# Two decoder layers on one core: output weights split ahead of the last gate and into dead tiles of the heads, the last gate by halves of its contraction, the early pool kept open

## The chip, the cores and the metric

The kernel runs on one core of a Trainium2 chip. The metric is the time of one execution in microseconds (us) on the device; the lower the better.

## What is computed

A trunk of two layers over 1024 tokens of width 1024, in float32. Each layer is `h = h + rmsnorm(mixer(rmsnorm(h)))`, and each mixer ends in a gate and an output projection:

```python
# layer 0: 16 heads of 64 in each of three dilated window groups
y = o.reshape(B, S, DIL_WIDTH).astype(h.dtype) * jax.nn.silu(gate)
return y @ w_out
# layer 1: 8 differential heads, v of width 128
y = o.reshape(B, S, DIFF_WIDTH) * jax.nn.silu(gate)
return y @ w_out
```

The part of interest is the turn at each layer's end: the last gate projection, the last heads, `y @ w_out`, and the norm behind it.

## The kernel before

**Numbers.** A float32 product is made of three matmuls: each operand is split into a high part (a ScalarE cast, `split`, L184) and a low part (a subtraction on VectorE or GpSimd in turn, `low`, L122). XH and XL, 128 x 8 x 1024, hold the transposed activations' high and low parts; slice kt is the kt-th 128 rows of the contraction (eight slices).

**Filler.** The heads run step by step, and between their steps `fill.at` lets a generator issue projection work: the projections of later heads (qk), then the late gates (`late_gates`, psum banks tagged "pj"), then `out_early`. TensorE's order is thus written out in the program; on the other engines, SyncE's list of transfers among them, a scheduler sets it by its own times. SyncE ("SP") issues every transfer, in one queue, in order.

**out_early.** Once the last gate has read XH and XL, finished branch outputs y are loaded over them (`load_y`, from the DRAM tensor y_d). With kt 0 to 3 (EARLY = 4) there, the first half of the output projection runs for eight token blocks n in two halves c, 12 matmuls each, in psum tiles `pe`. Each `pe` is copied by ScalarE into the tile `part`, which is stored over the slices of XH and XL that it has used up. The last two blocks (n = 6 and 7; HELD = 2) come after the last head. Then `po` takes kt 4 to 6 for block 0, for blocks 1 and 2, and at last kt 7 and the norm block by block (`out_rest`). Weights of kt are loaded into `raw` (two buffers), then split: kt 0 to 2 and 4 to 6 into the three buffers of `w_tiles` (tags "wh", "wl"; tiles print as wh and wl), kt 3 into "rh" of the early pool, kt 7 into a pool of its own (both print as owh and owl).

**What a turn waits for.** kt 0 to 2 share their three buffers with the weights of the last gates, and kt 4 to 6 share them with kt 0 to 2, so they can be split only when the last `pe` has been issued. In layer 0 the last y (`combine`) comes out of the softmax denominators by a chain: st_d, js, wt_d, twelve loads `wb`, the products on VectorE, the casts to XH and XL.

Of the kernel before, what the change touches and what calls it, by code (L numbers as in the profile page):

```python
# [10 lines left out]
F32 = mybir.dt.float32  # L11
# [81 lines left out]
def trunk(ctx: ExitStack, tc: tile.TileContext, a: dict, out: bass.AP):  # L93
# [177 lines left out]
    def project(o, wh, wl, tok):  # L271
        k = 0
        for kt in range(KT):
            for l, r_ in ((wh, XH), (wh, XL), (wl, XH)):
                nc.tensor.matmul(o, lhsT=l[:, kt, :], rhs=r_[:, kt, tok], start=k == 0, stop=k == 3 * KT - 1)  # L275
                k += 1
                yield 512

    def gate_units(pool, layer, w, fs, eng=None):
# [21 lines left out]
    def late_gates(pool, layer, w, fs):  # L301

        s = pool.tile([P, len(fs), T], F32, tag="r", name="sil", bufs=3 - layer)
        for v in gate_units(pool, layer, w, fs):
# [51 lines left out]

    stored = set()
# [28 lines left out]
    def out_weights(w, kt, tiles):  # L386
        raw = raw_tile([P, D])
        nc.sync.dma_start(raw, w[ts(kt), :])
        split(*tiles, raw)
        return tiles  # L390

# [11 lines left out]
    def out_early(pool, layer, w, held):  # L403

        ws = []
        for kt in range(EARLY):
            while (layer, kt) not in stored:
                yield None
            load_y(layer, kt)
            tiles = w_tiles([P, D]) if kt < 3 else [  # L410
                pool.tile([P, D], F32R, tag="rh", name=t) for t in ("owh", "owl")]
            ws.append(out_weights(w, kt, tiles))
        for n in range(NB):
            t = pool.tile([P, D], F32, tag="r", name="part", bufs=3 - layer)
            for c in range(2):
# [8 lines left out]
                nc.scalar.copy(t[:, ts(c, 512)], bank)  # L424
            for c, o in enumerate(partial(n)):
                nc.sync.dma_start(o, quarters(t[:, ts(c, 512)]))
        for kt in range(EARLY, KT - 1):
            held[kt] = out_weights(w, kt, w_tiles([P, D]))
        banks = held["banks"] = out_banks(0)
        for kt in range(EARLY, KT - 1):  # L430
# [3 lines left out]
            yield from out_block(0, banks, kt, *held[kt], kt == EARLY, False)  # L434

    def out_rest(pool, w, held, finish, early=None):

        held[KT - 1] = out_weights(
            w, KT - 1, [pool.tile([P, D], F32R, tag=t, name=t) for t in ("owh", "owl")])
# [88 lines left out]
    early0 = tc.tile_pool(name="early0", bufs=2, side="right")  # L528
    with tc.tile_pool(name="l0", bufs=2) as lp, early0 as ep:
# [196 lines left out]
        def filler0():  # L726
            for i, (pr, g) in enumerate(units):
                yield from qk_unit(ep, i, a["dil_qk"][i], SUB[g])
            if LATE0:
                yield from late_gates(ep, 0, a["dil_g"], range(8 - LATE0, 8))  # L730
# [12 lines left out]
        for i in range(nst + LAG_P):  # L743
            if i < nst:
# [10 lines left out]
                hd.scores(c)  # L755
                fill.at((3 * i + 1) / 24)
# [18 lines left out]
    with tc.tile_pool(name="ow0", bufs=1, side="right", reuse_waits="tile") as owp, \  # L775
            tc.tile_pool(name="o0", bufs=2, reuse_waits="tile") as op:
# [10 lines left out]
        def values1(pool, v2, weights=(wp, ("wh", "wl")), **kw):  # L787

            for parts in v_weights(*weights, a["diff_v"][v2], 256, 4, nc.vector):
# [20 lines left out]
        with tc.tile_pool(name="v1", bufs=3) as vp:  # L810
            ones = keep.tile([P, 1], F32, name="ones")
            nc.vector.memset(ones, 1.0)
            subln = keep.tile([P, 1], F32, name="subln")
            nc.sync.dma_start(subln, a["diff_subln"][0].rearrange("(d o) -> d o", o=1))
            nc.vector.tensor_scalar_mul(subln, subln, (1.0 - LAMBDA_INIT) * SQ_SHIFT)

            lqk = []
            for nm_ in ("q1", "k1", "q2", "k2"):
                t = vp.tile([P, HD], F32, tag="l" + nm_, name="l" + nm_, bufs=1)
                nc.sync.dma_start(t, a["diff_lambda_" + nm_][0].partition_broadcast(P))  # L820
                lqk.append(t)
            lsum = vp.tile([P, 2], F32, tag="lsum", name="lsum", bufs=1)
            for i in range(2):
                nc.vector.tensor_tensor_reduce(
                    lqk[2 * i], lqk[2 * i], lqk[2 * i + 1], 1.0, 0.0, ALU.mult, ALU.add, lsum[:, i : i + 1])
            nc.scalar.activation(lsum, lsum, AF.Exp)
            neg_lam = keep.tile([P, 1], F32, name="neg_lam")
            nc.vector.tensor_sub(neg_lam, lsum[:, 0:1], lsum[:, 1:2])
            nc.vector.tensor_scalar(neg_lam, neg_lam, LAMBDA_INIT, -1.0, ALU.add, ALU.mult)


            v = values1(vp, 0, (vp, ("vwh", "vwl")), tag="v")

            def first_weights():
                next(v)
                next(v)

            last = out_rest(owp, a["dil_w_out"][0], held, finish0, first_weights)
# [232 lines left out]
```

## Time and profile before

| | |
|---|---|
| median of three runs | 2046.3 us (2044.1 to 2049.32) |
| profiled execution, its own time | 2049.16 us |
| its span, first to last instruction | 2047.3 us |
| TensorE busy | 1911.4 us, 93% of the span |
| VectorE, ScalarE, GpSimd busy | 56%, 43%, 30% |
| mean granted TensorE clock | 0.975 of 2.4 GHz |

The difference of 1.9 us between the execution's time and its span lies outside the instructions. Where TensorE is busy nearly all the time, the stretches in which it isn't are those to read: slice 24 of 40 (1177 to 1228 us) shows 6 tenths, and the last ones 8.

### The profile page before, as it was taken

Reading aid. Unit: us, or ns where it says so; the run is one execution under the profiler, and the core shown is the slowest. Engines: PE = TensorE matmul, PEld = TensorE weight load, DVE = VectorE, ACT = ScalarE, POOL = GpSimd, SP = SyncE. Lnnn points to the kernel's source line nnn. Section 1 sums busy time; section 2 is a strip of 40 time slices with the busy share of each in tenths; the row PEclk is TensorE's granted clock in tenths of the full one; section 3 lists DMA queues with packets and bytes.
Section 4 is the critical chain, followed back from the end, with each engine's and each line's share of the span. In section 5 each row is a group of like instructions: output and inputs, shape, how many; then the busy total and the mean of one; then the engine's idle time right before and its main releaser. Section 6 shows DMA issues by size and latency. Waiting matters only on the chain.

```text
span 2047.3 us, 28864 instructions
## 1 busy us (share of the span) xinstructions
PE 1911.4 (93%) x10008; PEld 1598.6 (78%) x10008; DVE 1145.4 (56%) x2771; ACT 886.6 (43%) x2055; POOL 617.5 (30%) x386
## 2 busy tenths in 40 slices
PE   6999999999999999999999969899999899999888
PEld 4788888888787787788787848688879788887776
DVE  3311122146776767676767655570066877777626
ACT  3312122135555555555555555341245455546522
POOL 2000000143443434353535330230561534433121
PEclk8999999999999999999999979899999999999999
DMA  5424244277696969696969697542446565555643
GB/s 207 145 93 138 99 146 161 102 222 231 198 298 192 296 190 304 182 301 191 299 197 297 195 328 227 183 172 97 142 154 190 165 196 162 195 183 177 239 155 124
DMA packets 218018, 397.90 MB, mean 194 GB/s; under 512 B 40976, under 2 KB 123408, under 8 KB 217872
## 3 DMA queue, kind: packets, MB, share of 16 engines
q1 hardware_dynamic: 217872, 396.04, 60.7%
q8 instruction: 80, 1.31, 0.3%
q14 instruction: 66, 0.54, 0.1%
HBM read 254.87 MB, written 132.71 MB: 189 GB/s over the span
## 4 chain that ended last, share of the span: by engine, by line
PE 67%; DVE 11%; DMA 10%; ACT 4%; POOL 3%; issue 3%; SPq 1%; POOLq 0%; DVEq 0%; ACTq 0%
PE pqk L275 25%; PE pv L213 16%; PE pg L275 7%; PE po L377 3%; PE sc L576 3%; DMA wb<-wt_d 2%; PE sc L894 2%; PE up L626 2%; PE pe L420 2%; PE tp L599 2%; PE ob L945 2%; DVE u L649 1%; DMA st_d<-st 1%; POOL r L252 1%; DVE pm L897 1%
## 5 line engine op out<-in xcount | busy, mean ns | idle before, releaser
L275 PE MATMUL pqk<-XL,wh 128*128 128x512 f32 x1024 | 423.1, 413 | 0.0
L275 PE MATMUL pqk<-XH,wl 128*128 128x512 f32 x1024 | 411.8, 402 | 0.0
L275 PE MATMUL pqk<-XH,wh 128*128 128x512 f32 x1024 | 410.7, 401 | 0.9 <-DVE t L251 0.9
L122 POOL TENSOR_TENSOR wl<-raw,wh 128x1024 fp32r<-128x1024 f32 x41 | 98.5, 2402 | 612.1 <-ACT wh L184 612.1
L586 ACT ACTIVATE pm<-pm,st 128x128 f32<-128x128 f32 (+1 forms) x384 | 170.2, 444 | 155.9 <-DVE st L583 154.0
L275 PEld LDWEIGHTS pqk<-XH,wh 128*128 128x128 f32 x1024 | 194.9, 190 | 30.4 <-DVE t L251 1.9
L275 PEld LDWEIGHTS pqk<-XL,wh 128*128 128x128 f32 x1024 | 195.3, 191 | 27.6
L275 PEld LDWEIGHTS pqk<-XH,wl 128*128 128x128 f32 x1024 | 195.6, 191 | 27.2
L213 PE MATMUL pv<-vwh,XH 128*128 128x512 f32 (+1 forms) x448 | 173.8, 388 | 8.3 <-ACT XH L158 4.6
L250 POOL TENSOR_TENSOR r<-t 128x512 f32<-128x512 f32 x64 | 98.1, 1533 | 270.2 <-DVE t L249 269.2
L213 PE MATMUL pv<-vwl,XH 128*128 128x512 f32 (+1 forms) x448 | 172.4, 385 | 2.8 <-POOL vwl L122 2.8
L213 PE MATMUL pv<-vwh,XL 128*128 128x512 f32 (+1 forms) x448 | 172.6, 385 | 1.4 <-DVE XL L122 0.8
L184 ACT CAST wh<-raw 128x1024 fp32r<-128x1024 f32 x98 | 102.5, 1047 | 151.6 <-PE pqk L275 73.3
L122 DVE TENSOR_TENSOR wl<-raw,wh 128x1024 fp32r<-128x1024 f32 x57 | 76.0, 1333 | 147.6 <-ACT wh L184 147.3
L122 DVE TENSOR_TENSOR vs<-pv,vs 128x512 fp32r<-128x512 f32 x64 | 44.1, 689 | 200.5 <-ACT vs L495 187.9
L904 ACT ACTIVATE pm<-pm,mx 128x256 f32<-128x256 f32 (+7 forms) x128 | 99.4, 777 | 123.2 <-DVE mx L903 64.8
L122 DVE TENSOR_TENSOR pp<-tp,pp 128x512 fp32r<-128x512 f32 (+2 forms) x192 | 104.0, 541 | 80.8 <-ACT pp L603 79.2
L599 PE MATMUL tp<-ident,pm 128*128 128x128 f32 x560 | 96.3, 281 | 39.8 <-DVE pp L122 39.5
L599 PEld LDWEIGHTS tp<-ident,pm 128*128 128x128 f32 x560 | 73.1, 144 | 73.1 <-issue 36.5
L583 DVE CUSTOM_DVE_ANT_0 pm<-sc,masks 128x128 f32<-128x128 f32 (+1 forms) x384 | 118.7, 343 | 17.1 <-PE sc L576 15.7
L897 DVE CUSTOM_DVE_ANT_0 pm<-sc,md 128x512 f32<-128x512 f32 (+3 forms) x192 | 102.7, 551 | 31.1 <-PE sc L894 28.6
L495 ACT CAST vs<-pv 128x512 fp32r<-128x512 f32 x48 | 28.1, 586 | 187.2 <-PE pv L213 187.2
(516 smaller groups left out, 4441.0 us busy)
## 6 DMA issues: line engine op xcount, KB each, us to landing
qk_d<-rh SPq DMA_DIRECT2D x64, 512.0 KB
qk_d<-r SPq DMA_DIRECT2D x64, 512.0 KB
qh<-qk_d SPq DMA_DIRECT2D x128, 256.0 KB
ql<-qk_d SPq DMA_DIRECT2D x128, 256.0 KB
ka<-qk_d SPq DMA_DIRECT2D x64, 512.0 KB
v_d<-vs SPq DMA_DIRECT2D x48, 512.0 KB
raw<-in_dil_qk_dram SPq DMA_DIRECT2D x48, 512.0 KB
vt<-v_d SPq DMA_DIRECT2D x48, 512.0 KB
```

Source lines behind the costliest of these rows:

```text
L122: eng.tensor_tensor(o, full, hi.bitcast(F32), ALU.subtract)
L184: nc.scalar.copy(wh, raw)
L213: nc.tensor.matmul(o, lhsT=l, rhs=r_, start=first and k == 0, stop=last and k == 3 * KT - 1, skip_group_check=True)
L250: nc.gpsimd.tensor_sub(put(r[0]), nat(t1), nat(t2))
L275: nc.tensor.matmul(o, lhsT=l[:, kt, :], rhs=r_[:, kt, tok], start=k == 0, stop=k == 3 * KT - 1)
L377: nc.tensor.matmul(banks[c], lhsT=l[:, kt, ts(n)], rhs=r_[:, ts(c, 512)], start=first and k == 0, stop=last and k == 2,)
L576: nc.tensor.matmul(sc[:, cols], lhsT=q[:, ts(b)], rhs=kv, start=k == 0, stop=k == 1)
L583: nc.vector.tensor_tensor_reduce(pm[:, cols], sc[:, cols], m[:, m.shape[1] - w_ :], 1.0, 3.0e38, ALU.add, ALU.min, st[:, 0, j : j + 1])
L586: nc.scalar.activation(pm[:, cols], pm[:, cols], AF.Exp, bias=st[:, 0, j : j + 1], scale=-1.0, accum_out=st[:, 1, j : j + 1])
L599: nc.tensor.transpose(out=tp[:, ts(n)], in_=self.pb.pop((b, kb)), identity=ident)
L897: nc.vector.tensor_tensor_reduce(pm[:, k0:k1], sc[:, :w_], m_, 1.0, 3.0e38, ALU.add, ALU.min, mx[:, j : j + 1])
L904: nc.scalar.activation(pm[:, :wq], pm[:, :wq], AF.Exp, bias=mx[:, 0:1], scale=-1.0, accum_out=den)
```

## The change

1. `gate_units` opens both psum banks for the last gate f = 7 and projects kt 0 to 3 into both, then kt 4 to 7 into both (before: bank c = 0 over all kt, then c = 1). The number of matmuls is the same.
2. `prepare` issues loads and splits of the output weights kt 0 to 2 right behind the last gate's own split; kt 3 follows behind the gate.
3. `out_weights` picks tiles by kt: kt 0, 1, 3, 7 from `w_tiles`; kt 2 in the two "rh", kt 4 in "qh" and "ql", kt 5 in two "r", kt 6 in the two "ka" of the early pool, where the heads kept their operands. kt 4 to 6 are traced in front of block n = 6, once the last head's scores are issued; kt 7 behind the `pe` loop.
4. `part` is a tile of half the size, 128 x 512, with tag "t" (three buffers in layer 0, two in layer 1), in place of 128 x 1024 of tag "r".
5. The pools of kt 7 are gone; the early pool of layer 0 stays open till the first block of layer 1's values (`values1(0)`) is done, which takes its tiles from "pq" and `w_tiles`. The lambda of layer 1 is set up behind that, in the gates' stage.

```diff
+    def project(o, wh, wl, tok, kts=range(KT)):
...
+    def gate_units(pool, layer, w, fs, eng=None, prepare=None):
...
+            if prepare and f == fs[-1]:
+                prepare()
+                banks = [ps.tile([P, 512], F32, tag="pj", name="pg") for _ in range(2)]
+                for k0 in (0, EARLY):
+                    for c in range(2):
+                        yield from project(banks[c], wh, wl, ts(c, 512), range(k0, k0 + EARLY))
+                for c in range(2):
+                    yield f, c, banks[c]
+                return
...
+    def out_weights(pool, w, kt):
+
+        tags = {2: ("rh", "rh"), 4: ("qh", "ql"), 5: ("r", "r"), 6: ("ka", "ka")}
+        if kt in tags:
+            tiles = [pool.tile([P, D], F32 if t == "r" else F32R, tag=t, name="ow", bufs=2 if t != "r" else r_bufs[pool])
+                     for t in tags[kt]]
+            tiles = [t.bitcast(F32R) for t in tiles] if kt == 5 else tiles
+        else:
+            tiles = w_tiles([P, D])
         raw = raw_tile([P, D])
         nc.sync.dma_start(raw, w[ts(kt), :])
         split(*tiles, raw)
         return tiles
...
+    def out_early(pool, layer, w, ws):
+
+        ws[EARLY - 1] = out_weights(pool, w, EARLY - 1)
         for kt in range(EARLY):
             while (layer, kt) not in stored:
                 yield None
             load_y(layer, kt)
-            tiles = w_tiles([P, D]) if kt < 3 else [
-                pool.tile([P, D], F32R, tag="rh", name=t) for t in ("owh", "owl")]
-            ws.append(out_weights(w, kt, tiles))
         for n in range(NB):
-            t = pool.tile([P, D], F32, tag="r", name="part", bufs=3 - layer)
+            if n == NB - HELD:
+                while ("heads", layer) not in written:
+                    yield None
+                for kt in range(EARLY, KT - 1):
+                    ws[kt] = out_weights(pool, w, kt)
+            parts = []
...
-                nc.scalar.copy(t[:, ts(c, 512)], bank)
-            for c, o in enumerate(partial(n)):
-                nc.sync.dma_start(o, quarters(t[:, ts(c, 512)]))
-        for kt in range(EARLY, KT - 1):
-            held[kt] = out_weights(w, kt, w_tiles([P, D]))
-        banks = held["banks"] = out_banks(0)
+                t = pool.tile([P, 512], F32, tag="t", name="part", bufs=3 - layer)
+                nc.scalar.copy(t, bank)
+                parts.append(t)
+            for o, t in zip(partial(n), parts):
+                nc.sync.dma_start(o, quarters(t))
+        ws[KT - 1] = out_weights(pool, w, KT - 1)
+        banks = ws["banks"] = out_banks(0)
```

Three places show how the instructions move. In each row stand the line, the operation and out<-in with the buffer's number; "waits" lists the engines and transfer slots (DMAHW) whose work it waits for.

**Layer 0, SyncE, the y loads of kt 0 to 3.** Before, the first load (XH, kt 0) stands three rows ahead of this piece, and the weights of kt 2 (raw_11122) stand among the loads:

```order
L549 DMA vt_10878<-v0_d_59 128x4x128 [waits DMAHW3_49]
L394 DMA XL_79<-y_d0_63 128x1024 [waits DMAHW4_49]
L717 DMA sil_in_10861<-sil_d0_65 128x512 [waits DMAHW5_49,DVE_49]
L370 DMA y_d0_63<-u_9843 128x512 [waits DMAHW6_49,Activation_49]
L394 DMA XH_78<-y_d0_63 128x1024 [waits DMAHW7_49]
L394 DMA XL_79<-y_d0_63 128x1024 [waits DMAHW0_49]
L370 DMA y_d0_63<-u_9433 128x512 [waits DMAHW1_49,DVE_49]
L394 DMA XH_78<-y_d0_63 128x1024 [waits DMAHW2_49,PE_49]
L394 DMA XL_79<-y_d0_63 128x1024 [waits DMAHW3_49]
L388 DMA raw_11122<-in_dil_w_out_dram 128x1024 [waits DMAHW4_49]
L394 DMA XH_78<-y_d0_63 128x1024 [waits DMAHW5_49,PE_49]
```

Now, where raw_11122 holds the weights of kt 3:

```order
L737 DMA sil_in_10880<-sil_d0_65 128x512 [waits DMAHW2_49,DVE_49]
L569 DMA vt_10897<-v0_d_59 128x4x128 [waits DMAHW3_49,PE_49]
L379 DMA y_d0_63<-u_9843 128x512 [waits DMAHW4_49,Activation_49]
L379 DMA y_d0_63<-u_9433 128x512 [waits DMAHW5_49,DVE_49]
L569 DMA vt_10897<-v0_d_59 128x4x128 [waits DMAHW6_49]
L416 DMA raw_11122<-in_dil_w_out_dram 128x1024 [waits DMAHW7_49]
L397 DMA XH_78<-y_d0_63 128x1024 [waits DMAHW0_49]
L397 DMA XL_79<-y_d0_63 128x1024 [waits DMAHW1_49]
```

All eight loads stand together now, behind two stores and kt 3's weights; kt 2's weights went some 35 rows up, among the twelve `wb` loads of the previous head pair.

**Layer 0, ScalarE, behind the last head.** Before, with the casts of kt 4, 5, 6 and 7 (wh_11835, wh_11841, wh_11847, owh_11910) behind the last `part` copies:

```order
L424 COPY part_11773<-pe_11774 128x512 [waits DMAHW4_49,DMAHW3_49,PE_49]
L363 CAST XH_78<-u_10589 128x512 [waits DVE_49]
L424 COPY part_11773<-pe_11788 128x512 [waits PE_49]
L424 COPY part_11804<-pe_11805 128x512 [waits DMAHW1_49,DMAHW0_49,PE_49]
L184 CAST wh_11835<-raw_11837 128x1024 [waits PE_49]
L363 CAST XH_78<-u_10589 128x512 [waits DVE_49]
L184 CAST wh_11841<-raw_11843 128x1024 [waits PE_49]
L424 COPY part_11804<-pe_11819 128x512 [waits PE_49]
L184 CAST wh_11847<-raw_11849 128x1024 [waits DMAHW1_49,Pool_49]
L184 CAST owh_11910<-raw_11912 128x1024 [waits DMAHW6_49,DMAHW2_49]
```

Now, with the casts of kt 7 (wh_11861) and of layer 1's values (wh_12137):

```order
L444 COPY part_11810<-pe_11797 128x512 [waits DMAHW4_49,PE_49]
L372 CAST XH_78<-u_10589 128x512 [waits DVE_49]
L444 COPY part_11825<-pe_11812 128x512 [waits DMAHW4_49,PE_49]
L444 COPY part_11842<-pe_11829 128x512 [waits DMAHW5_49,PE_49,Activation_49]
L372 CAST XH_78<-u_10589 128x512 [waits DVE_49]
L184 CAST wh_11861<-raw_11863 128x1024 [waits DMAHW1_49,PE_49]
L184 CAST wh_12137<-raw_12139 128x1024 [waits DMAHW1_49,PE_49]
L444 COPY part_11857<-pe_11844 128x512 [waits DMAHW6_49,PE_49,Activation_49]
```

The casts of kt 4 to 6 moved up between the exponentials of the last two heads; every `part` copy now waits for a store of an earlier half.

**Layer 1, ScalarE, behind the last head.** Before, with the casts of kt 4, 5, 6 and 7:

```order
L424 COPY part_18579<-pe_18594 128x512 [waits PE_49]
L424 COPY part_18610<-pe_18611 128x512 [waits DMAHW1_49,DMAHW2_49,PE_49,Activation_49]
L184 CAST wh_18641<-raw_18643 128x1024 [waits PE_49]
L184 CAST wh_18647<-raw_18649 128x1024 [waits PE_49]
L424 COPY part_18610<-pe_18625 128x512 [waits PE_49]
L184 CAST wh_18653<-raw_18655 128x1024 [waits DMAHW3_49]
L184 CAST owh_18693<-raw_18695 128x1024 [waits DMAHW4_49]
```

Now only kt 7's cast (wh_18671) is left among the copies:

```order
L444 COPY part_18620<-pe_18607 128x512 [waits DMAHW3_49,PE_49,Activation_49]
L444 COPY part_18635<-pe_18622 128x512 [waits DMAHW4_49,PE_49,Activation_49]
L184 CAST wh_18671<-raw_18673 128x1024 [waits DMAHW6_49,PE_49]
L444 COPY part_18652<-pe_18639 128x512 [waits DMAHW1_49,Activation_49]
L444 COPY part_18667<-pe_18654 128x512 [waits DMAHW2_49,PE_49,Activation_49]
```

The casts of kt 4 to 6 stand 24 to 30 rows higher, between the exponentials of head 7.

## Rows read from the trace of the kernel before

**Rows 1.** Windows: us, each engine's busy us (instructions), granted clock, DMA share, GB/s.

```profile
1170.00:1180.00 10.00, 9.21 (x52) 7.35 (x51) 7.43 (x23) 6.62 (x18) 4.93 (x3) 1.00 0.44 118
...
1210.00:1220.00 10.00, 3.60 (x11) 2.60 (x11) 1.38 (x2) 1.73 (x3) 1.29 (x1) 0.50 1.03 419
...
1240.00:1245.00 5.00, 5.00 (x32) 4.36 (x31) 2.94 (x11) 3.50 (x11) 0.00 (x0) 1.00 1.07 278
...
1255.00:1260.00 5.00, 5.00 (x30) 4.29 (x29) 3.42 (x17) 4.45 (x16) 0.00 (x0) 1.00 0.59 156
```

**Rows 2.** Timeline, PE, layer 0's first turn: start us, us, instruction, idle before.

```profile
1211.93 0.79 PE L420 MATMUL pe<-wh,XH 128*128 128x512 f32 x1 [2.06 <-DMA XH<-y_d]
...
1218.69 0.79 PE L420 MATMUL pe<-wh,XH 128*128 128x512 f32 x1 [4.47 <-ACT wh L184]
...
1224.38 0.63 PE L420 MATMUL pe<-owh,XL 128*128 128x512 f32 x1
...
1250.37 0.30 PE L576 MATMUL sc<-ka,qh 128*128 128x128 f32 x1 [0.79 <-DMA XH<-part]
```

**Rows 3.** Chain that ended last, 1195 to 1262 us: start us, us, what.

```profile
1204.28 7.60 DMA XH<-y_d
1211.90 9.43 DMA raw<-in_dil_w_out_dram
...
1238.67 6.63 DMA qh<-qk_d
1245.37 4.90 DMA XH<-part
```

**Rows 4.** Timeline, SP, the same stretch.

```profile
1210.67 0.32 SPq L394 DMA_DIRECT2D XL<-y_d  x1
...
1244.48 0.33 SPq L394 DMA_DIRECT2D XL<-y_d  x1
```

**Rows 5.** Timeline, ACT: casts and copies named in the text.

```profile
1217.59 1.04 ACT L184 CAST wh<-raw 128x1024 fp32r<-128x1024 f32 x1 [6.22 <-DMA raw<-in_dil_w_out_dram]
...
1249.38 0.59 ACT L424 COPY part<-pe 128x512 f32<-128x512 f32 x1
...
1286.83 0.62 ACT L363 CAST XH<-u 128x512 fp32r<-128x512 f32 x1 [3.03 <-DVE u L721]
...
1893.82 1.05 ACT L184 CAST owh<-raw 128x1024 fp32r<-128x1024 f32 x1 [3.64 <-DMA raw<-in_diff_w_out_dram]
```

**Rows 6.** Timeline, PE, layer 0's second turn.

```profile
1284.65 0.40 PE L377 MATMUL po<-wh,XH 128*128 128x512 f32 x1
...
1288.93 0.80 PE L377 MATMUL po<-wh,XH 128*128 128x512 f32 x1 [1.89 <-ACT part L424]
...
1296.24 0.80 PE L377 MATMUL po<-wh,XH 128*128 128x512 f32 x1 [3.60 <-ACT wh L184]
...
1309.88 0.40 PE L377 MATMUL po<-owh,XH 128*128 128x512 f32 x1
```

**Rows 7.** Chain, layer 0's second turn: start us, us, what.

```profile
1280.59 3.74 DMA sil_in<-sil_d
```

**Rows 8.** Timeline, PE, layer 1: head 7's first scores, then the last turn.

```profile
1900.48 0.47 PE L894 MATMUL sc<-ka,qh 128*128 128x128 f32 x1 [5.95 <-DMA raw<-in_diff_w_out_dram]
...
1983.16 0.40 PE L377 MATMUL po<-wh,XH 128*128 128x512 f32 x1
1984.81 0.51 PE L377 MATMUL po<-wl,XH 128*128 128x512 f32 x1 [1.25 <-POOL wl L122]
...
1990.50 0.49 PE L377 MATMUL po<-wh,XH 128*128 128x512 f32 x1 [2.86 <-ACT wh L184]
1992.98 0.79 PE L377 MATMUL po<-wl,XH 128*128 128x512 f32 x1 [1.99 <-POOL wl L122]
...
2037.12 0.40 PE L377 MATMUL po<-owh,XL 128*128 128x512 f32 x1
```

**Rows 9.** Chain, layer 1's end: start us, us, what, matmuls.

```profile
1969.12 12.12 PE pe L420 x52
```

More of the change, by code (lines that the diff above doesn't have):

```diff
@@ L269, in heads_in @@
         return qh, ql, ka
[L271 to L276, printed above, removed]
+    def project(o, wh, wl, tok, kts=range(KT)):
+        for kt in kts:
+            for k, (l, r_) in enumerate(((wh, XH), (wh, XL), (wl, XH))):
+                nc.tensor.matmul(o, lhsT=l[:, kt, :], rhs=r_[:, kt, tok],
+                                 start=kt == 0 and k == 0, stop=kt == KT - 1 and k == 2)
                 yield 512
-    def gate_units(pool, layer, w, fs, eng=None):
+    def gate_units(pool, layer, w, fs, eng=None, prepare=None):
         for f in fs:
@@ L401, in quarters @@
         return t.rearrange("p (j q) -> p j q", j=EARLY)
-    def out_early(pool, layer, w, held):
-        ws = []
+    def out_weights(pool, w, kt):
[6 more added lines that the diff above has]
+            tiles = w_tiles([P, D])
+        raw = raw_tile([P, D])
+        nc.sync.dma_start(raw, w[ts(kt), :])
+        split(*tiles, raw)
+        return tiles
+    def out_early(pool, layer, w, ws):
+        ws[EARLY - 1] = out_weights(pool, w, EARLY - 1)
         for kt in range(EARLY):
@@ L433, in out_early, with out_rest @@
             load_y(layer, kt)
[L434 to L439, printed above, removed]
+            yield from out_block(0, banks, kt, *ws[kt], kt == EARLY, False)
+    def out_rest(held, finish, early=None):
         later, bs = [], {0: held["banks"]}
@@ L728, in filler0, with prepare @@
                 yield from qk_unit(ep, i, a["dil_qk"][i], SUB[g])
-            if LATE0:
-                yield from late_gates(ep, 0, a["dil_g"], range(8 - LATE0, 8))
+            def prepare():
+                for kt in range(EARLY - 1):
+                    held[kt] = out_weights(ep, a["dil_w_out"][0], kt)
+            yield from late_gates(ep, 0, a["dil_g"], range(8 - LATE0, 8), prepare)
             nc.sync.dma_start(cos, a["norm_post"][0].partition_broadcast(P))
@@ L755, in trunk @@
                 hd.scores(c)
+                if i == nst - 1:
+                    written.add(("heads", 0))
                 fill.at((3 * i + 1) / 24)
@@ L808, in values1 @@
             written.add(("v", v2))
[L810 to L834, printed above, removed]
-                next(v)
-                next(v)
-            last = out_rest(owp, a["dil_w_out"][0], held, finish0, first_weights)
-            nc.sync.dma_start(cos, a["cos"])
-            nc.sync.dma_start(sin, a["sin"])
-            for n, f in zip((48, 48, 48, 0), last):
-                for _ in range(n):
-                    next(v)
-                f()
-            run(v)
-            for v2 in range(1, 4 - len(VALUES_AFTER)):
-                run(values1(vp, v2, tag="v"))
-            run(gates(vp, 1, a["diff_g"], range(8 - LATE1)))
@@ L905, in scores @@
                     pm[:, :wq], pm[:, :wq], AF.Exp, bias=mx[:, 0:1], scale=-1.0, accum_out=den)
+                if self.h == 7 and i == NB - 1 and s:
+                    written.add(("heads", 1))
                 if s == 0:
@@ L999, in filler1, with prepare @@
                     yield from values1(ep, VALUES_AFTER[h], tag="r", bufs=2)
+            def prepare():
+                for kt in range(EARLY - 1):
+                    held[kt] = out_weights(ep, a["diff_w_out"][0], kt)
             for f in range(8 - LATE1, 8):
[L1001 removed]
+                yield from late_gates(ep, 1, a["diff_g"], (f,), prepare if f == 7 else None)
             nc.sync.dma_start(cos, a["norm_post"][1].partition_broadcast(P))
```

68 lines of the change are left out of this document (49 added, 19 removed).

## The prediction, made before the changed kernel ran

> **What bounds the kernel now.** TensorE is busy 93% of the span, and its program is the same before and after: the same matmuls in the same order, but for the order of kt within the last gate. A change in time can only come out of its waits and of the slow clock behind them. So I read first the page's 40 slices, then TensorE's timeline where a slice falls short, then the chain that ended last there, and the transfer and ScalarE timelines for what released it. Three stretches come out. In layer 0's first turn the granted clock falls to 0.50 of 2.4 GHz, that is 1.2 GHz, for ten us in which TensorE is busy 3.60 us [rows 1], with waits for y loads and for kt 2's weights [rows 2]. In layer 0's second turn the first `po` matmuls wait for a `part` copy and for weights [rows 6]. In layer 1 the last turn waits for weights three times, 1.25 + 2.86 + 1.99 = 6.1 us [rows 8].
>
> **Layer 0, first turn: 0 us.** Before, the first `pe` block starts its last matmul at 1224.38, behind 4.47 us of waiting for kt 2's weights [rows 2], whose raw load held ScalarE for 6.22 us [rows 5]. Now the weights of kt 0 to 2 are ready; what remains is the y loads. They don't come earlier: the first of the eight now stands behind both y_d stores and kt 3's weights. The queue is full there, with a DMA share of 1.03 and 1.07 [rows 1], and SyncE issues as transfers land, so a load's place in the bytes decides. Ahead of the last y load (XL, kt 3), kt 3's 512 KB are added and kt 2's 512 KB are gone, to a stretch where the DMA share is 0.44 [rows 1]. It is issued at 1210.67 [rows 4]; between kt 2's weights, issued ahead of it and cast at 1217.59 [rows 5], and kt 3's, which land at 1211.90 + 9.43 = 1221.3 [rows 3], I put its landing at 1219.5. The block would then end 4.5 us earlier. But the queue stays full, and at 1250.37 TensorE waits for a transfer at the start of the last head [rows 2]; the chain runs through two transfers, 6.63 and 4.90 us, up to it [rows 3]. Ahead of that head's loads the list is the same, plus XL of kt 6, which stood behind them at 1244.48 [rows 4]: 512 KB at 278 GB/s [rows 1] is 1.8 us. So the 4.5 us are given back as a longer wait at the last head. Bounds: -4.5 (nothing given back) to +1.8; I take 0, since the row at 1250.37 shows the queue already ending last.
>
> **Layer 0, heads behind it: +1 us.** The casts of kt 4, 5 and 6 now stand on ScalarE between the exponentials of the last two heads. Queued behind each are those exponentials, and TensorE's transposes wait for them. kt 6's raw load is issued behind the last head's loads in a full queue. Nothing (the load landed) to 3.6 us (the other wait of this kind, 3.64 [rows 5]). The half tiles add a wait too: the sixth `part` copy, at 1249.38 [rows 5], now needs the third half's store, issued at 1245.37 and landed 4.90 later, at 1250.3 [rows 3]: 0.9 us. I take 1 for both.
>
> **Layer 0, second turn: -6.5 us.** Before, from the first `po` matmul at 1284.65 to kt 7's first at 1309.88 are 25.2 us [rows 6] for 54 matmuls (three blocks, three kt, six each). At 12.12/52 = 0.233 us each [rows 9] they need 12.6, so at most 12.7 can be won. The weights of kt 4 to 6 are ready now, but the copies aren't: block 6's second copy needs the buffer of block 5's first half, whose store stands behind the twelve `wb` loads and the last `sil_in`, about where that load was issued, 1280.59 [rows 7]. The load, of the same 256 KB, took 3.74 us: 1284.2 or so for the store. The copy ends at 1284.8, the last `pe` half (12 matmuls, 2.8 us) at 1287.6. Its own copy stands behind the cast to XH (1286.83 [rows 5], 0.6 us) and two weight casts of 1.05: it ends at about 1290.1, against 1288.93 before [rows 6]. Three matmuls of the first bank are done by then; 51 remain, 11.9 us, with no further wait. A pause costs clock as well: in layer 1's turn 9.5 us are lost (below) of which 6.1 are waits, so 0.55 us per us; for a pause of some 2.5 us that is 1.4. kt 7 starts at 1290.1 + 11.9 + 1.4 = 1303.4: 6.5 us won. Bounds: if the store takes 7.60 us as a load did in the full queue [rows 3], it is 3.9 later and 2.6 are won; 12.7 if the copies wait for nothing.
>
> **Layer 1, heads: 0.** The wait of 5.95 us at 1900.48 [rows 8] is named for kt 3's raw load, but that TensorE instruction reads only qh and ka; I read it as their loads in a backlog. kt 3's load is issued earlier now, but kt 4's takes its place among head 7's loads, so the bytes are the same. If kt 3's load was the cause in itself, -5.95. ScalarE no longer stands 3.64 us for kt 3 [rows 5]; its new casts wait for head 7's operands to be read; two of them held in front of an exponential would be 2 us. I take 0 between the two.
>
> **Layer 1, last turn: -8.5 us.** 192 matmuls run from 1983.16 to 2037.12 + 0.23 [rows 8], 54.2 us; at 0.233 they need 44.7. 9.5 can be won. kt 7's cast can start when the last `pe` half has read kt 0, some 1.5 us ahead of `po`, and is wanted 36 matmuls or 8.4 us later, so it hides. The last copy follows the last `pe` matmul by 0.6 us while three `po` matmuls take 0.7. I leave 1 us for copies that wait for a store. If a store takes 7.60 us in place of 3.74, `po` starts up to 3.9 late: 5.6 won. Bounds -5.6 to -9.5.
>
> **Small: +0.5 us.** The last gate's second bank is wanted twelve matmuls earlier, so it waits for the projection's copies out of it; the lambda's exponential adds table loads in the gates' stage, under matmuls; the values' tiles have two buffers for three. What hides the first is the head steps between the gate's matmuls; bare, each is a copy or a table load of 1 us or so. 0 to 2 us.
>
> **Sum.** 0 + 1 - 6.5 + 0 - 8.5 + 0.5 = -13.5. The profiled execution took 2049.16 (span 2047.3 and 1.9 around it), so its like would take 2035.7; it lies 2.9 above the median of 2046.3, on which scale the forecast is **2032.8**. A measurement here tells 0.3%, 6.1 us, from no change.
>
> **Rivals.** *The loads land soon.* If a transfer's time is its own and not the queue's, the first turn keeps its 4.5 us, layer 0's copies come 3 us earlier and layer 1's on time: 2046.3 - 4.5 - 9.5 - 9.5 + 1 = 2023.8. Against it: 512 KB took 7.60 and 9.43 us [rows 3]. In favour: 3.74 for 256 KB once the share is down to 0.59 or so [rows 1, 7]. The Trainium skill (DMA: Bandwidth & Descriptors, section on the anatomy of one DMA) gives about 2.0 us plus the bytes at 436 GB/s, which would be 3.2 us for a y load; by it the estimate would be this rival's, and this trace disagrees for the first turn (7.60) and is nearer to it in the second (3.74 against 2.6).
>
> *Layer 0 gains nothing.* The `part` halves wait for their stores block after block, and the second turn starts as late as its weights did. Then only layer 1's 8.5 is left, less 1.5: 2039.3. For it: three buffers of half a tile in place of three whole ones, with stores of 4.90 us against 2.8 us a half.
>
> *Slower: the casts block ScalarE.* Eight casts of output weights (kt 2, 4, 5, 6 in either layer) now stand in front of exponentials. If each held the heads as long as the 3.64 us at 1893.82 [rows 5], that is 29.1 us; less 15.0 of the two turns, 2060. It decides from (15.0 + 6.1)/8 = 2.6 us a cast. Against it: the raw loads are issued well ahead, and TensorE was not shown waiting for ScalarE behind that cast.
>
> **How the numbers follow.** Forecast 0.60, loads soon 0.13, layer 0 nothing 0.16, slower 0.11. The forecast's bounds: best -4.5 + 0 - 12.7 - 5.95 - 9.5 = -32.7, worst 1.8 + 3.6 - 2.6 + 2 - 5.6 + 2 = +1.2; all ends together are unlikely, so it lies within 2024 to 2040. The range takes in the first two rivals: 2019 to 2043. Faster: 0.58 + 0.13 + 0.08; same: 0.02 + 0.07 + 0.03; slower 0.09.
>
> **What would show it.** Right: no wait for weights behind either last `pe`; the first turn's block ends near 1220, and the wait at the last head has grown to about 4 us; `po` of layer 0 waits once, for a copy, and kt 7 starts some 6 us earlier; `po` of layer 1 runs its 192 matmuls in about 45 us. Wrong: TensorE waiting for `part` copies before block 6, ScalarE idle for raw loads between exponentials, or the last head on time after a first turn that ends early.

## The result, and the profile after

The changed kernel takes 2032.3 us (median of 4 runs, 2031.09 to 2036.69), the kernel before on the same chip 2046.9 (2044.1 to 2049.32): a ratio of 0.9933, interval 0.9913 to 0.9953. The forecast was 2032.8. The profiled execution took 2031.38 us with a span of 2029.5, 17.8 less than before; TensorE's busy time fell from 1911.4 to 1905.9 us, and its granted clock rose from 0.975 to 0.981.

TensorE's timeline of the changed kernel, the rows that answer to [rows 2, 6, 8]:

```profile
1212.20 0.79 PE L439 MATMUL pe<-wh,XH 128*128 128x512 f32 x1 [3.19 <-DMA XH<-y_d]
...
1219.97 0.47 PE L439 MATMUL pe<-wh,XH 128*128 128x512 f32 x1 [0.77 <-DMA XH<-y_d]
...
1221.12 0.50 PE L439 MATMUL pe<-wh,XL 128*128 128x512 f32 x1
...
1238.88 0.44 PE L596 MATMUL sc<-ka,qh 128*128 128x128 f32 x1 [5.99 <-DMA ka<-qk_d]
...
1288.74 0.80 PE L439 MATMUL pe<-wh,XH 128*128 128x512 f32 x1 [5.24 <-ACT part L444]
...
1293.74 0.63 PE L386 MATMUL po<-ow,XH 128*128 128x512 f32 x2
...
1306.64 0.39 PE L386 MATMUL po<-wh,XH 128*128 128x512 f32 x1
...
1889.50 0.30 PE L921 MATMUL sc<-ka,qh 128*128 128x128 f32 x1 [3.79 <-issue]
...
1974.59 0.72 PE L386 MATMUL po<-ow,XH 128*128 128x512 f32 x2 [0.64 <-ACT part L444]
...
2019.35 0.40 PE L386 MATMUL po<-wh,XL 128*128 128x512 f32 x1
```

No `po` waits for weights any more. The first `pe` block ends at 1221.12, 3.3 us earlier, but a new wait of 5.99 us stands at head 46, one head ahead of the last. In the second turn the only wait, 5.24 us, is one of a `pe` for a `part` copy; from the first `po` to kt 7's are 12.9 us. In layer 1 the 192 products run from 1974.59 to the end without a gap.

SyncE's timeline says why the wait stands at head 46. Its operands are qh, ql and ka. Before:

```profile
1217.63 0.34 SPq L394 DMA_DIRECT2D XH<-y_d  x1
...
1220.15 1.67 SPq L266 DMA_DIRECT2D qh<-qk_d  x2
1221.91 1.19 SPq L266 DMA_DIRECT2D ql<-qk_d  x2
1223.15 0.58 SPq L268 DMA_DIRECT2D ka<-qk_d  x1
...
1224.77 0.46 SPq L394 DMA_DIRECT2D XL<-y_d  x1
1225.28 0.42 SPq L394 DMA_DIRECT2D XH<-y_d  x1
1225.94 0.51 SPq L394 DMA_DIRECT2D XL<-y_d  x1
1227.08 1.51 SPq L370 DMA_DIRECT2D y_d<-u  x2
1230.05 0.88 SPq L388 DMA_DIRECT2D raw<-in_dil_w_out_dram  x2
```

Now:

```profile
1217.35 0.36 SPq L416 DMA_DIRECT2D raw<-in_dil_w_out_dram  x1
1218.64 0.34 SPq L320 DMA_DIRECT2D sil_d<-sil  x1
1219.90 0.32 SPq L397 DMA_DIRECT2D XH<-y_d  x1
1221.10 0.32 SPq L397 DMA_DIRECT2D XL<-y_d  x1
1221.51 0.38 SPq L397 DMA_DIRECT2D XH<-y_d  x1
...
1222.42 0.43 SPq L397 DMA_DIRECT2D XL<-y_d  x1
...
1223.43 0.57 SPq L416 DMA_DIRECT2D raw<-in_dil_w_out_dram  x1
1224.09 1.36 SPq L266 DMA_DIRECT2D qh<-qk_d  x2
1226.83 2.47 SPq L266 DMA_DIRECT2D ql<-qk_d  x2
1229.35 0.58 SPq L268 DMA_DIRECT2D ka<-qk_d  x1
```

The weights of kt 4 and 5 (raw) and three of the four y loads of kt 4 and 5 stood behind that head's ka load before: five transfers of 512 KB, 2.6 MB, have moved ahead of it. (The two stores y_d<-u, 256 KB each, have moved as well; they stay ahead of the operands in late_queue below, where the wait is gone.)

The chain that ended last, up to the last `pe` half (block n = 7, c = 1), answers to [rows 7]:

```profile
1284.89 3.14 DMA XH<-part
...
1288.11 0.59 ACT part L444
...
1288.74 5.16 PE pe L439 x12
```

The store took 3.14 us where I had taken 3.74, and was issued 4.3 us later than I had taken; 2.3 of these had been lost before the last `up`, a head's output product in layer 0.

### The profile page after: what moved, and what is told of

It is laid out like the page before. It is cut to its first block, busy times and chain, and to the rows that moved or that the text cites. A ratio compares the mean times of both kernels' runs of the same rounds, so it can differ in the third digit from the quotient of the medians.

```text
span 2029.5 us, 28888 instructions
## 1 busy us (share of the span) xinstructions
PE 1905.9 (94%) x10008; PEld 1594.5 (79%) x10008; DVE 1143.0 (56%) x2771; ACT 888.0 (44%) x2057; POOL 618.0 (30%) x386
## 4 chain that ended last, share of the span: by engine, by line
PE 62%; DMA 13%; DVE 12%; ACT 4%; POOL 4%; issue 3%; SPq 1%; POOLq 0%; DVEq 0%; ACTq 0%
PE pqk L274 22%; PE pv L213 16%; PE pg L274 8%; PE po L386 4%; PE sc L921 2%; PE pe L439 2%; PE up L646 2%; PE sc L596 2%; DMA wb<-wt_d 2%; PE ob L974 2%; DMA st_d<-st 2%; PE tp L619 2%; DVE u L669 1%; POOL r L252 1%; DVE pm L924 1%
## 5 line engine op out<-in xcount | busy, mean ns | idle before, releaser
L122 POOL TENSOR_TENSOR wl<-raw,wh 128x1024 fp32r<-128x1024 f32 x35 | 84.0, 2400 | 500.6 <-ACT wh L184 500.6
L122 DVE TENSOR_TENSOR wl<-raw,wh 128x1024 fp32r<-128x1024 f32 x61 | 82.0, 1345 | 149.1 <-ACT wh L184 148.6
L213 PE MATMUL pv<-vwh,XH 128*128 128x512 f32 x384 | 155.8, 406 | 7.0 <-ACT XH L158 4.0
L213 PE MATMUL pv<-vwl,XH 128*128 128x512 f32 x384 | 154.9, 403 | 2.8 <-POOL vwl L122 2.8
L213 PE MATMUL pv<-vwh,XL 128*128 128x512 f32 x384 | 154.8, 403 | 0.9 <-DVE XL L122 0.3
L619 PEld LDWEIGHTS tp<-ident,pm 128*128 128x128 f32 x560 | 72.6, 143 | 73.5 <-issue 34.2
```

The costliest lines, as they stand in the source:

```text
L122: eng.tensor_tensor(o, full, hi.bitcast(F32), ALU.subtract)
L213: nc.tensor.matmul(o, lhsT=l, rhs=r_, start=first and k == 0, stop=last and k == 3 * KT - 1, skip_group_check=True)
L619: nc.tensor.transpose(out=tp[:, ts(n)], in_=self.pb.pop((b, kb)), identity=ident)
```

## The experiments

Places on TensorE's timeline are compared in one table. **end**: start of the last matmul of layer 0's first `pe` block. **A**: from there to head 46's first score. **B**: on to the last `up` (layer 0's last output product). **C**: to the last `pe`. **D**: to the last `po` ahead of kt 7. **E**: from layer 0's last `po` to the last transposes of x, the input of layer 1's projections. **F**: in layer 1, from the last head's projection to the end of the last gate. **G**: from the last score to the last head's last output product. **H**: the 192 products behind the last `pe`. All in us; the ratio to the kernel before is the timed one, with its interval.

```
                    end      A     B     C     D     E     F     G     H   ratio
before            1224.4  12.8  33.7  13.6  25.2  27.5  60.2  20.7  54.2
changed           1221.1  17.8  34.2  20.4  12.9  23.4  57.2  24.0  45.8  0.9933 [0.9913, 0.9953]
after_again       1223.9  18.8  34.6  20.2  12.9  23.3  56.8  24.0  45.5  0.9924 [0.9906, 0.9943]
late_layer1       1229.7  18.7  35.3  20.9  13.1  23.3  54.9  20.7  53.1  0.9955 [0.9937, 0.9972]
late_layer0       1222.5  17.8  35.3  15.8  23.8  27.6  56.6  22.5  45.1  0.9984 [0.9971, 0.9997]
gate_by_banks     1226.0  18.7  36.6  19.5  12.9  23.4  56.9  22.4  45.2  0.9925 [0.9907, 0.9944]
late_queue        1221.7  12.3  34.2  12.8  20.3  23.4  53.3  22.6  45.1  0.9877 [0.9855, 0.9898]
part_act_queue    1223.2  21.3  36.7  12.9  18.0  23.4  58.8  25.1  45.6  0.9954 [0.9936, 0.9973]
late_casts        1226.4  17.9  34.7  21.5  12.9  23.3  56.6  25.2  45.1  0.9930 [0.9909, 0.9951]
all_three         1223.0  11.5  37.4  12.8  15.2  23.4  52.5  26.9  45.6  0.9877 [0.9857, 0.9897]
late_queue_vector 1220.6  11.6  35.2  12.9  22.3  23.4  57.3  21.4  45.2  0.9876 [0.9852, 0.9901]
late_queue_parts  1225.4  11.6  37.1  12.8  17.1  23.4  52.7  22.7  45.1  0.9867 [0.9843, 0.9892]
kt2_after_gate    1227.8  17.7  35.7  19.4  12.9  23.3  56.8  22.5  45.1  0.9939 [0.9914, 0.9963]
own_value_tiles   1228.6  18.5  35.6  21.4  13.1  22.5  56.4  22.4  45.1  0.9929 [0.9905, 0.9953]
```

One execution each: places that no edit touches differ by 1 to 3 us (G is 22.4 to 24.0 in runs with the same layer 1, B 34.2 to 36.6 with the same heads), and `end` by 9: it carries the drift of 1200 us, small differences between executions that pile up.

**after_again.** The changed kernel once more.

> The changed kernel once more, for a second trace of it. Theory (the queue paces layer 0's first turn, copies that wait for stores pace the second): 2032 us; again a wait of 5 to 6 us for ka in front of the head at 1237 of before, again a wait of about 5 us for a part copy in front of the last block, the 192 po matmuls of layer 1 in 45 us. Rival (much of the 14 us is the luck of one execution): the waits in other places, and stretches that differ by over 2 us from the first trace.

The gain is there again (2036.1 us against 2049.8), and the profile shows the same waits: 7.03 us at head 46, 5.15 in the second turn, with C, D and H within 0.4 us.

**late_layer1.** kt 4 to 6 of layer 1 are split in `w_tiles` behind the last `pe`.

```diff
+        if layer == 1:
+            tags = {2: ("rh", "rh"), 7: ("qh", "ql")}
...
-            if n == NB - HELD:
+            if n == NB - HELD and layer != 1:
...
+        if layer == 1:
+            for kt in range(EARLY, KT - 1):
+                ws[kt] = out_weights(pool, w, kt, layer)
```

> In layer 1 alone the output weights of kt 4 to 6 go back to the three shared buffers behind the last pe block, and kt 7 to qh and ql; all the rest is the changed kernel. Theory (the last turn's 8.5 us come from these splits): po of layer 1 waits for weights three times again, its 192 matmuls take 53 to 54 us, and the kernel is 8.5 us slower than the changed one, 2041. Rival (the gain at the end comes from the part halves and the earlier y loads): within 2 us of the changed kernel, 2032 to 2034.

H is 53.1 again, with the waits for weights back, but the total rises by 5.5 us only (2041.7 against 2036.1): F and G fall by 1.9 and 3.3 us. So early splits in layer 1 gain 7.7 in H and cost in front of it.

**late_layer0.** The same in layer 0, which needs tiles of their own ("rh", "ka") for the values' weights.

> In layer 0 alone the output weights of kt 4 to 6 go back to the three shared buffers behind the last pe block, kt 7 to qh and ql, the first values' weights to rh and ka. Theory (the second turn's 6.5 us come from these splits): from the issue of the last sil_in to kt 7's first matmul it takes 6 to 7 us more than in the changed kernel, and the kernel is 6.5 us slower, 2039. Rival (the copies that wait for stores bound this turn either way): at most 2 us slower, 2034.

It takes 11.0 us more than after_again. C and D together are 39.6, near those of before (38.8), against 33.1: 6.5 us, as expected. Another 4.3 are in E, a place of which the prediction says nothing. (The profiled execution, 2042.9 us, is one of the shortest of its twelve, so the places don't add up to the 11.0 of the medians there.)

**gate_by_banks.** The last gate again one bank after the other.

```diff
-                for k0 in (0, EARLY):
-                    for c in range(2):
-                        yield from project(banks[c], wh, wl, ts(c, 512), range(k0, k0 + EARLY))
+                for c in range(2):
+                    yield from project(banks[c], wh, wl, ts(c, 512))
```

> The last gate runs bank by bank over all kt again, in both layers; all the rest is the changed kernel. Theory (the y loads are paced by the full transfer queue, not by when XH comes free): the first pe matmul of layer 0 starts within 1 us of the changed kernel's, and the time is within 1.5 us of it, 2031 to 2034. Rival (the loads wait for the gate's reads): the first pe block ends 12 matmuls, 2.8 us, later, and the kernel is 2.8 to 4.5 us slower, 2035 to 2037.

The time doesn't change (2035.5 against 2036.1), but that doesn't settle it: each of the two intervals reaches some 4 us to either side, and the rival asked for 2.8 or more. The place doesn't either. Measured from layer 0's last head projection, the first block ends after 47.4 us, against 45.2 and 45.6, later as the rival says; but runs that keep the gate's order reach 47.6 (late_casts). A gain or loss by the gate's order isn't shown.

**late_queue.** Loads of kt 4 to 6 behind the last head's ka load on SyncE.

```diff
+        loaded[0] = nc.sync.dma_start(ka.bitcast(F32), qk_d[unit, 1, h].rearrange("l e f t -> (l e f) t"))
...
+                with tc.issue_after(loaded[0].ins):
+                    for kt in range(EARLY, KT - 1):
+                        ws[kt] = out_weights(pool, w, kt)
...
+            with tc.issue_after(loaded[0].ins):
+                load_y(layer, kt)
```

> The changed kernel, but the loads of the weights and of the y rows of kt4 to kt6 are issued on SyncE's queue behind the ka load of the last head, in both layers; in the changed kernel some 3 MB of them stand ahead of the operands of head 46 (qh 1224.09, ka 1229.35, against 1220.15 and 1223.15 before). Theory: the 6 us that TensorE waits for ka at head 46 (5.99 and 7.03 in the two profiles of the changed kernel, none before) are the price of that place in the queue. Then the wait falls to under 1 us, the stretch from the block's last product to head 46's first score goes from 17.8-18.8 us to 12.5-13.5, and the time falls by 4 to 6 us. Rival 1: the time of layer 0's first block is given back whatever the queue does, because the operands of head 46 come from a store that is late itself: the stretch stays at 17-19 us and the time within 1.5 us. Rival 2: the weights of kt4 to kt6 now come too late for their splits, and a wait of 3 us or more stands ahead of the first product behind the last partial one in one layer; the time is then the same or up to 3 us more.

The wait at head 46 is gone, and A falls from 18.8 to 12.3 us. Layer 1 had the same thing in small: F falls by 3.5. C and D together stay (33.1); the wait for the `part` copy has moved onto the first `po`. The ratio falls by 0.005 to 0.006, 10 to 11 us, twice what I expected, and is clearly below the changed kernel's. SyncE and TensorE of this kernel:

```profile
1221.01 1.12 SPq L266 DMA_DIRECT2D qh<-qk_d  x2
1222.23 1.19 SPq L266 DMA_DIRECT2D ql<-qk_d  x2
1223.46 0.58 SPq L268 DMA_DIRECT2D ka<-qk_d  x1
```

```profile
1233.97 0.22 PE L599 MATMUL sc<-ka,qh 128*128 128x128 f32 x1
...
1286.54 1.22 PE L387 MATMUL po<-ow,XH 128*128 128x512 f32 x2 [5.16 <-ACT part L446]
```

The operands are issued 3 to 6 us earlier and head 46 starts without a wait. None of the three weights is late (the 5.16 us stand for a `part` copy): rival 2 is out.

**part_act_queue.** Stores of `part` on ScalarE's queue (`nc.scalar.dma_start`).

> The changed kernel, but the stores of the partial sums (part to XH, XL) are issued on ScalarE's queue and not on SyncE's. Theory: the copies of the last partial sums wait for the stores before them, which stand on SyncE's queue behind the loads of wb and sil_in (copies waited 3.01 for a store of part at 1288.11 in layer 0, TensorE 5.24 for the copy at 1288.74). Then TensorE's wait of 5 us ahead of the last partial products of layer 0 falls to under 2 us, the stretch from the last up to the last pe from 20.2-20.4 us to 16-17.5, and of it 3 to 4 us stay in the total. Rival 1: the stores take as long on another queue, since the transfer itself is what lasts (wb and sil_in fill the DMA engines): the stretch stays at 19.5 us or more and the time within 1 us. Rival 2: the stores cost ScalarE the time to issue them (32 in each layer, between exps that TensorE waits for), and the heads behind become longer by more than is won: slower by 1 us or more.

C falls to 12.9, further than the theory said, but D rises to 18.0, B by 2.1 and A by 2.5 us; the ratio rises by 0.002 to 0.003, some 5 us, at the edge of what the intervals tell apart. ScalarE's timeline shows why A grows:

```profile
1228.20 0.19 ACT L606 ACTIVATION_READ_ACCUMULATOR pm<-pm,st 128x1 f32 x1
1239.31 0.67 ACTq L447 DMA_DIRECT2D XH<-part  x1
1240.02 0.48 ACT L623 CAST pp<-tp 128x384 fp32r<-128x384 f32 x1 [11.64 <-DMA ql<-qk_d]
```

ScalarE stood 11.64 us in front of its first store, until a transfer of ql had landed, and TensorE then waited 8.06 us for pp, the transposed probabilities. In the program's order that store waits for five transfer slots, where one on SyncE's own queue waits for one or none: issued from another queue, it is made to wait here for transfers that SyncE issued earlier. Issuing it takes only 0.67, so rival 2 was right about the engine and not about the price.

**late_casts.** In layer 1, splits of kt 4 to 6 behind the last exp.

> The changed kernel, but in layer 1 the weights of kt4 to kt6 are loaded and split behind the last exp of the last head, not between its exps. Theory: the casts (1.2 us each on ScalarE) in front of the exps are what makes the stretch from the last score to the last head's last output product 23.9-24.0 us in the changed kernel against 20.7 before (and 20.7 with the splits moved to the end of layer 1): it goes back to about 20.7, the 192 products behind the last partial one stay at 45.1-45.8 us, and the time falls by 3 us. Rival 1: splits that late are not done when the last partial product is, and the 192 products take 49 us or more: no gain, or up to 2 us slower. Rival 2: the 3.3 us come from the partial sums' copies on ScalarE and not from the casts: the stretch stays at 23.5 us or more and the time within 1 us.

Missed: G is 25.2, more than the 24.0 that it should have cured. So the casts in front of the exps (1.04 us each in the trace, not 1.2) aren't what holds head 7. Nor are the `part` copies of rival 2, whose numbers came true: late_layer1 keeps them, and its G is 20.7. VectorE's timeline of this kernel, then GpSimd's:

```profile
1940.71 2.32 DVE L1007 TENSOR_TENSOR nr<-nr,nd 128x4 f32<-128x4 f32 x1 [0.90 <-POOL nr L1006]
1942.95 1.21 DVE L122 TENSOR_TENSOR ow<-raw,ow 128x1024 fp32r<-128x1024 f32 x1
```

```profile
1940.65 2.36 POOL L122 TENSOR_TENSOR ow<-raw,ow 128x1024 fp32r<-128x1024 f32 x1
```

A step on 128x4 numbers, 0.16 us in late_layer1, lasts 2.32 us, until GpSimd's subtraction of the weights ends; TensorE then waits 2.76 us for `pl`, the low part of transposed probabilities. The changed kernel has it too, GpSimd's row first:

```profile
1929.37 2.39 POOL L122 TENSOR_TENSOR ow<-raw,ow 128x1024 fp32r<-128x1024 f32 x1
```

```profile
1929.96 2.08 DVE L988 TENSOR_SCALAR sq<-os__18280 128x512 f32<-128x512 f32 x1
...
1932.03 0.68 DVE L122 TENSOR_TENSOR pl<-tp,ph 128x512 fp32r<-128x512 f32 x1
```

Without such a subtraction beside them, in late_layer1:

```profile
1934.49 0.43 DVE L993 TENSOR_SCALAR sq<-os__18280 128x512 f32<-128x512 f32 x1
...
1942.43 0.16 DVE L1010 TENSOR_TENSOR nr<-nr,nd 128x4 f32<-128x4 f32 x1 [0.43 <-POOL nr L1009]
```

**all_three.** The three edits together.

> The three edits together: loads of kt4 to kt6 behind the last head's ka load, stores of the partial sums on ScalarE's queue, and layer 1's splits of kt4 to kt6 behind the last exp. If each of the three theories holds and their stretches don't overlap, the sum is 4 to 6, 3 to 4 and 3 us, so 10 to 13 us below the changed kernel, about 2022 us and a ratio near 0.986 to 0.988. Rival: the waits are one resource (the DMA queue), and what one edit wins the next wait takes: 3 to 6 us in all.

2025.0 us, the same as late_queue alone. That lies where the sum put it, but not for its reason: late_queue by itself gave 10 to 11 us, and the other two edits add nothing. D is 5.1 us shorter than in late_queue, B 3.2 and G 4.3 longer. The rival is right in that what one edit wins the next wait takes, and wrong in its 3 to 6 us; that the waits are one resource isn't shown, since G already grew with late_casts alone.

**late_queue_vector.** late_queue, with the low halves of kt 4 to 6 subtracted by VectorE.

```diff
-        split(*tiles, raw)
+        split(*tiles, raw, eng and (alt(), eng)[1])
...
-                        ws[kt] = out_weights(pool, w, kt)
+                        ws[kt] = out_weights(pool, w, kt, nc.vector)
```

> late_queue, but the low halves of the weights of kt4 to kt6 are subtracted on VectorE in both layers (in late_queue every second subtraction is GpSimd's). Theory: what made layer 1's last head longer is neither the casts nor the copies on ScalarE but GpSimd's subtractions of 128x1024 (2.38 us): a step of VectorE that began inside one lasted until that one's end (pm of 128x896 3.28 us in place of 1.15, mx of 128x1 1.10 in place of 0.16, u of 64x256 2.00 in place of 0.42 in late_queue; sq 2.08 in place of 0.43 in the changed kernel). Without them the stretch from the last score to the last head's last output product falls from 22.6 to 20.7-21.7 us, layer 0's from the last score to the last up from 13.1 to 11.5-12.3, and the time by 1 to 3 us. Rival: three subtractions of 1.2 us on VectorE stand in front of the same scores, so nothing is won: both stretches stay within 0.5 us and the time within 1 us.

Half right. G falls to 21.4 us, in the range given, and no step of VectorE there is stretched; with one trace, and G moving by 1.6 between runs alike, the 1.2 us are a sign and no proof. But layer 0's stretch from the last score to the last up stays at 13.1, so GpSimd wasn't its cause; and in F a wait of 3.9 us for ka is back in this run, though SyncE's order is the same there, which no run explains. In layer 0 the wait ahead of `po` grew from 5.16 to 7.32 us: SyncE's order of stores and `wb` loads came out another there, which the edit didn't intend. The total is late_queue's.

**late_queue_parts.** late_queue, with layer 0's stores of n = 5 to 7 on ScalarE's queue.

> late_queue, but in layer 0 the stores of the partial sums of n = 5, 6 and 7 are issued on ScalarE's queue. Theory: with part_act_queue the copies no longer waited for stores behind wb and sil_in, and what made that kernel slower was its first store of n = 0, behind which ScalarE stood 11.64 us while the operands of head 46 were still loading; n = 5 to 7 come after those loads. Then the wait of 5.2 us ahead of layer 0's products behind the last pe falls to 2.4 us or less, the stretch from the last pe to kt7's first product from 20.8 to 15-17.5 us, and the time by 3 to 5.5 us. Rival 1: a store on ScalarE stands in front of the exps and copies of the last head's combine and makes them late: the stretch from the last up to the last pe grows by as much as the other shrinks, and the time stays within 1 us. Rival 2: it is slower by 2 us or more, since a store there waits 5 us or more for an earlier transfer.

D falls to 17.1 as expected, with a wait of 2.65 us where 2.4 or less was expected, and the wait for slots is avoided. B grew by 2.9 us: there `pe` waited 1.52 and 1.21 us for `part` copies, the first behind a cast for which ScalarE stood 5.36 us because its raw load had not landed. The time is late_queue's within the interval. The stores in question are issued after B, so I can't say that the edit caused this; the gain isn't shown.

**kt2_after_gate.** In layer 0 kt 2's weights come behind the last gate, with kt 3's.

> The changed kernel, but in layer 0 kt2's weights are loaded and split with kt3's, behind the last gate's products; only kt0 and kt1 stay ahead of them. Theory: the end of layer 0's last gate came 4.8 and 6.1 us later than before in the two profiles of the changed kernel because kt2's load stands among the loads of wb (1176.58) and its split among head 44's steps; then the gate's end comes 3 to 5 us earlier (about 1205), the first partial product with it, and the block's twelfth product stays 9 us behind its first or takes up to 4 more, since kt2 and kt3 land one behind the other: time between 4 us less and 1 us less. Rival 1: the delay has nothing to do with kt2 (the order of the products in the gate, or the drift of one run): the gate's end stays at 1208-1210, kt2 and kt3 come later, and the time is the same or up to 5 us more.

The theory fell: the gate's end comes at 1210.7, no earlier than in the changed kernel (1208.6 and 1209.9; before 1203.8). The block needs 12.9 us in place of 8.9, as foreseen, and the time isn't measurably different. Part of the lateness is drift: layer 0's last head projection, ahead of kt 2's load, stands at 1174.0 before, at 1175.9 and 1178.3 in the changed kernel, and at 1178.6 here. From there to the gate's end it is 29.8 us before, 32.7 and 31.6 in the changed kernel, and 32.1 here.

**own_value_tiles.** The values' weights in "rh", "qh", "ql".

> The changed kernel, but the weights of the values computed behind layer 0's last products stand in the tiles of rh, qh and ql, as they did before, and not in the shared wh and wl. Theory: the shared tiles are what shortened the stretch from layer 0's last output product to the last transposes of x from 27.5 to 23.4 us, since the next gates' splits then wait for the tiles and no longer stand on VectorE ahead of xn; with own tiles the stretch is 27.5 us again, and the time is 4 us more than the changed kernel's, with all other stretches the same. Rival: the 4 us come from the earlier end of the products (other steps of the normalisation lie differently), and the stretch stays at 23.4 and the time within 1 us.

This fell too: E is 22.5 us. VectorE's rows around stretch E tell the two cases apart by the number of gate weights split there. Before:

```profile
1342.36 1.28 DVE L122 TENSOR_TENSOR wl<-raw,wh 128x1024 fp32r<-128x1024 f32 x1 [0.95 <-ACT wh L184]
...
1347.22 1.21 DVE L122 TENSOR_TENSOR wl<-raw,wh 128x1024 fp32r<-128x1024 f32 x1
...
1350.61 1.21 DVE L122 TENSOR_TENSOR wl<-raw,wh 128x1024 fp32r<-128x1024 f32 x1
```

The changed kernel has one there, at 1343.47, and own_value_tiles one, at 1357.70, with two done at 1316.49 and 1321.20; late_layer0 has three again, at 1347.93 to 1356.20, and its E is 27.6. What `before` and late_layer0 share is kt 4 to 6 in `w_tiles`, not the values' tiles: three buffers come free together when the products end, and three splits then stand among the normalisations. In both a step of the normalisation is stretched besides, xn, 3.25 and 3.26 us in place of 1.28, under GpSimd's xb<-pn,xb. Before:

```profile
1357.33 3.25 DVE L144 SCALAR_TENSOR_TENSOR xn<-xb,r,sin 128x1024 f32<-128x1024 f32 x1
```

```profile
1357.13 2.37 POOL L474 TENSOR_TENSOR xb<-pn,xb 128x1024 f32<-128x1024 f32 x1
```

That these make up E's 4 us is read from the rows; no run changes them alone.

## Why the prediction was right, step by step

- **Layer 0, first turn: 0.** The block's end was right (forecast near 1220, measured 1221.1), and that it is given back. Measured from layer 0's last head projection, to leave the drift out, the block ends after 45.2 and 45.6 us against 50.4: 5.2 and 4.8 won where 4.5 were forecast. A gives back 5.0 and 6.0, so the 0 came out within about 1 us. The place was wrong: head 46, not the last head. The step that failed is "Ahead of that head's loads the list is the same": I read the list ahead of the last head only. late_queue shows the queue's order as the cause.
- **Heads behind it: +1.** B grew by 0.5 and 0.9 us. That fits, but B moves by more than this between runs, and no run tells which of the two waits it was.
- **Second turn: -6.5.** Measured -5.5 and -5.7 (C + D), and +6.5 when undone. The mechanism was as told: block 6's second copy waits for a store behind `wb` and `sil_in`, and the last `pe` half for that copy. It ends at 1288.7 and not at 1284.8, and TensorE stands 5.24 us ahead of the half; the other pause, 2.5 us of `po` for the last copy, didn't come.
- **Layer 1, heads: 0.** F fell by 3.0 and G grew by 3.3 us (by 1.7 or 1.8 in four other runs with the same layer 1), so the sum is near right and neither part was foreseen. That the wait at 1900.48 [rows 8] was a backlog and not kt 3's load in itself is borne out by three of the four runs with moved loads, where F is 52.5 to 53.3 us; late_queue_vector, with 57.3, doesn't fit.
- **Layer 1, last turn: -8.5.** Measured -8.4 and -8.7; late_layer1 undoes 7.7. kt 7 is wanted 54 matmuls behind the first `po`, not 36, which only helps.
- **Small: +0.5.** No run shows it: it is less than the times can tell.
- **Not in the sum:** E, -4.1 us. With it the places from layer 0's last head projection on come to some 17.5 us in both traces, 4 more than forecast. The two profiled spans differ by 17.8; after_again's span is 2033.1, 14.2 less than before, with 4.4 us of drift ahead of the first place and 1.6 the other way in layer 1's projections, which no edit touches; and the medians differ by 14.6. So the forecast of 2032.8 came closer to 2032.3 than its parts allow: that is luck.
- **Rivals.** Loads don't land soon (7 us at head 46), and a reading in that rival's favour was wrong: the load of 3.74 us in the kernel before ran at a DMA share of 0.89 (window 1280 to 1285 us), not 0.59. The formula of the Trainium skill quoted there stands in a section on transfers issued from GpSimd, while these are SyncE's; the measured 7.60 and 9.43 us decide. Layer 0 does gain. The casts didn't hold the heads (late_casts: the rows show VectorE held at head 7, beside GpSimd's half of the split).

Open: why the stretch from layer 0's last head projection to its last gate's end is longer, 29.8 us before and 31.1 to 33.6 in all later traces. TensorE's waits between 1150 and 1213 us, those for y loads left out, sum to 7.6 us before and 8.4 now, and neither the order of the gate nor kt 2's place changed it.

## What to carry to other kernels

Making work ready earlier moves its loads up a queue that is served in order; list what stands behind them there, for each consumer that follows and not only for the one that waits today. Here the change won 0.7%, and putting its loads behind the next two heads' operands won another 0.5%. And a helper that alternates engines may not be neutral where the other engine's chain is on the path: a step there can be held for a whole instruction.

## What the runs showed of the hardware

**GpSimd's subtraction stops some steps of VectorE.** Rows above: 0.43 becomes 2.08, 0.16 becomes 2.32, each ending within 0.3 us of GpSimd's end; yet `pl<-tp,ph`, with one operand in PSUM, takes its usual 0.68 us beside one (late_queue, 1922.60, under GpSimd's 1921.67 to 1924.28). With GpSimd's subtractions moved to VectorE (late_queue_vector) the same two steps take 0.42 and 0.15. The Trainium skill (SBUF — State Buffer, section "Who interferes with whom") says that VectorE instructions with two SBUF inputs, or in a two-port mode, contend with GpSimd for one port pair, and that the loser waits for the whole instruction; these rows agree, though the trace doesn't tell the mode of the sq step, which has one SBUF input.

**A pause costs clock behind it.** In late_queue, behind the 5.16 us wait, the windows (us, PE busy, other engines, granted clock, DMA share, GB/s) read:

```profile
1287.00:1291.00 4.00, 4.00 (x11) 3.03 (x11) 2.12 (x4) 1.02 (x2) 0.00 (x0) 0.50 0.75 184
1292.00:1301.00 9.00, 9.00 (x40) 7.26 (x39) 1.23 (x1) 0.91 (x1) 0.00 (x0) 1.00 0.85 345
```

At 0.50 (1.2 GHz) a `po` matmul takes 0.43 us against 0.23 at 1.00. D is 20.3 us for 12.6 us of products: 5.3 of pause and 2.4 of slow clock, 0.5 us for each us waited, near the 0.55 that the prediction took from layer 1. But the cost doesn't grow with the pause: behind the 7.32 us wait of late_queue_vector, where D is 22.3, it is 2.2. So 0.55 us per us is no rate to carry to a pause of another length.
